# Gate projections of two sequence mixers: wide split products against plain products on four column quarters

## The chip, the cores and the metric

The kernel runs on one core of one Trainium2 chip. The metric is the time of one execution in device microseconds (us); lower is better. The core has a matrix engine (PE, with its weight loads listed apart as PEld), a vector engine (DVE), a scalar engine (ACT), a third elementwise engine (POOL) and a queue engine (SP) that issues most of the transfers. They run side by side and wait for one another at semaphores.

## The reference, cut to what matters

The program is a two-layer encoder trunk over 512 tokens of width 1024, in float32. Layer 0 mixes tokens with forgetting attention and differential attention, layer 1 with a chunkwise mLSTM. Each mixer reads the normalised input and, beside its large projections, a very narrow one: eight gate columns.

```python
xn = rms_norm(x, mix_norm[layer])              # x * rsqrt(mean(x^2) + eps) * gain
proj = xn @ w_in                               # 1024 -> some 3000 columns
# layer 0: ff is 8 of those columns, one for each forgetting head
log_f = log_sigmoid(ff + fox_bf)               # its running sum biases the attention logits
# layer 1: ig and fg are 4 columns each, one for each mLSTM head
i_pre = ig + b_i
log_f = log_sigmoid(fg + b_f)
```

The change concerns only how these 8 + 8 columns, 16 numbers for each token, are computed. Their later use (running sums, maxima, exponentials) stays.

## The kernel before, in words

**Layout.** x is held transposed, as eight tiles of 128 model dimensions by 512 tokens (`x0` to `x7`). A projection is a sum over these eight blocks k.

**Split products.** Float32 operands are split in two: a high part (`xh`, `wh`) in a reduced float type that the matrix engine takes at full rate, and the remainder (`xl`, `wl`). A large product is three matmuls: high times high, high times low, low times high. ACT makes the high part (a cast, line 285), DVE the low part (a subtraction, line 282). For x the gain of the norm is multiplied in at the same time (lines 604 and 605). The root of the mean square is divided out later, when a result is read from its bank (`rb`, the reciprocal root spread over the partitions).

**Weights.** A weight tile of 128 by 1024 arrives by a transfer in `raw`, is split into `wh` and `wl`, and is used by 24 matmuls. There are three `wh` and three `wl` buffers, and tiles take them in turn: a new `wl` waits until the products that read the tile three turns earlier have run.

**Order.** In both mixers a planner (class `Plan`) sets the order in which instructions are written. It holds assumed durations, priorities, and some times before which an item may not start (`after`); the memory work of layer 0 enters at such times (`MEM_AT` = 140 and 95). All engines run their own list in the order written, so one waiting instruction holds everything behind it on its engine.

**The gates.** `p_gate` adds one planner item for each k, of two matmuls: the gate weights against `xh[k]` (line 669) and against `xl[k]` (line 670). The gate weights are split as well, and high and low part lie side by side as columns of one `wh` buffer: 40 columns in layer 0 and 100 in layer 1, with gaps, so that each part begins at a multiple of 32. So there are 16 matmuls over 512 tokens in each layer. `gate_rows` then adds the rows of the two parts (lines 679 and 680), multiplies by `rb` (681) and adds the bias (682); in layer 1 it runs twice, for input and forget gate.

**Around them.** In layer 0 the gates stand among the first products of the program, between the products of the value projection of the differential heads (`dv`, lines 352 to 354, four blocks of 128 tokens at a time), while x is still being prepared. The root of layer 0 runs through lines 588 (sums), 484 to 489 (root), 559 (diagonal tiles) and 565 (two products that spread it). In layer 1 they follow the last product of layer 0's feed-forward block, and the mLSTM's value projection (lines 352 to 354 again) follows them; the norm sums are line 498.

**Other float32 products.** `weigh` of the differential heads (line 814) and of the forgetting heads (line 1033) multiply float32 tiles without a split. Line 1033 does so for two heads at once: 64 columns each, written to partitions 0 to 63 and 64 to 127 of one bank, with a position given for each product:

```python
for s in range(2):
    nc.tensor.matmul(ps[64 * s : 64 * s + 64, j * P : 512], v[j][:, c : c + 64], ...,
        start=(j == 0), stop=(j == 3), tile_position=(0, 64 * s))
```

Of the kernel before, what the change touches and what calls it, by code (L numbers as in the profile page):

```python
# [236 lines left out]
class Builder:  # L237
# [407 lines left out]
    def gate_weights(self, src, m, parts):  # L645

        nc = self.nc
        raw = self.til(self.sp, "gw", (P, 8, m), bufs=1)
# [9 lines left out]
    def p_gate(self, pl, weights, w, evac, kdeps=None, edeps=(), prio=0):  # L658

        st = {}  # L660
        last = None
        for k in range(KB8):

            def fn(k=k):
                if k == 0:
                    st["g"] = weights()
                    st["ps"] = self.bank("w")
                mm = self.nc.tensor.matmul
                mm(st["ps"][:w, :], st["g"][:, k, :], self.xh[k][:], start=(k == 0), stop=False)
                mm(st["ps"][:w, :], st["g"][:, k, :], self.xl[k][:], start=False, stop=(k == 7))  # L670
# [4 lines left out]
    def gate_rows(self, out, ps, hi, lo, n, bias):  # L675

        nc = self.nc
        t = self.til(self.sp, "sqt")[:n, :]
        nc.scalar.copy(t, ps[lo : lo + n, :])
        nc.vector.tensor_tensor(out=t, in0=ps[hi : hi + n, :], in1=t, op=ALU.add)  # L680
        nc.vector.tensor_tensor(out=t, in0=t, in1=self.rb[:n, :], op=ALU.mult)
        nc.vector.tensor_scalar(out=out, in0=t, scalar1=self.col(bias)[:n, :], scalar2=None, op0=ALU.add)
# [1647 lines left out]
```

## Time and profile before

| what | us |
|---|---|
| median of 3 runs (lowest, highest) | 1453.03 (1452.55, 1453.50) |
| the profiled execution, its whole time | 1452.78 |
| its span in the profile | 1451.0 |
| PE busy | 1435.7 (99%) |
| PEld busy | 1276.1 |
| DVE busy | 1223.3 (84%) |
| ACT busy | 992.0 (68%) |

The span is what the instructions of the trace cover; 1.78 us of the profiled execution lie around it. The granted clock of the matrix engine was 0.999. Rows of a timeline give the start in us from the span's start, the duration, the engine, the line, the operation, and the tiles written and read, with their shapes; in brackets stands the idle time before an instruction and what ended it. Matmuls overlap in their pipeline, so the spacing of their starts tells the rate, not the duration of one: a split product of 512 columns takes 0.39 us and the next starts some 0.23 us later. A float32 product without a split leaves two records for each instruction.

### The profile page before, as it was taken

What the parts mean: (1) busy time and instruction counts of PE and PEld (TensorE: products, weight loads), DVE (VectorE), ACT (ScalarE), POOL (GpSimd) and SP (SyncE); (2) the same over time, 40 slices, a digit from 0 to 9 for tenths busy, and PEclk for the clock granted to TensorE, in tenths of its full rate; (3) what the DMA queues carried; (4) which work ended last, traced back from release to release, by engine and by line L of the source; (5) the groups of instructions that cost most, each with busy time, mean ns of one, the idle gap of its engine ahead of it and who ended that gap; (6) DMA issues with size and microseconds to landing.
All of it is one profiled execution on the core that took longest, in us unless ns stands there. A gap on an engine that the chain in (4) does not pass through costs nothing.

```text
span 1451.0 us, 23997 instructions
## 1 busy us (share of the span) xinstructions
PE 1435.7 (99%) x8989; PEld 1276.1 (88%) x8989; DVE 1223.3 (84%) x2171; ACT 992.0 (68%) x1782; POOL 74.7 (5%) x116
## 2 busy tenths in 40 slices
PE   9999999999999999999999999999999999999998
PEld 7888788998889999999888788899888999999987
DVE  7789987877899988888769888887779999888974
ACT  7689766655677777777547676566566777777764
POOL 0001120000000000000000100000000000000000
PEclk9999999999999999999999999999999999999999
DMA  5222336752246655552233323656314666565322
GB/s 201 87 74 73 117 118 209 184 167 79 95 135 163 180 161 158 151 161 74 84 106 109 121 90 102 189 146 174 131 52 124 175 161 174 153 167 153 102 71 75
DMA packets 71062, 190.37 MB, mean 131 GB/s; under 512 B 7825, under 2 KB 7954, under 8 KB 70946
## 3 DMA queue, kind: packets, MB, share of 16 engines
q1 hardware_dynamic: 63170, 162.30, 33.5%
q0 software_dynamic: 7200, 26.22, 10.5%
q8 instruction: 70, 1.15, 0.3%
q14 instruction: 46, 0.38, 0.1%
q10 hardware_dynamic: 576, 0.33, 0.1%
HBM read 186.69 MB, written 2.13 MB: 130 GB/s over the span
## 4 chain that ended last, share of the span: by engine, by line
PE 79%; DVE 12%; ACT 4%; issue 3%; DMA 1%; POOL 0%; DVEq 0%; SPq 0%; POOLq 0%; ACTq 0%
PE acc L291 14%; PE acc L292 14%; PE acc L293 14%; PE w L291 6%; PE w L293 6%; PE w L292 6%; PE s L291 3%; PE s L293 3%; PE s L292 3%; DVE wl L282 2%; PE acc L352 2%; PE acc L354 2%; PE acc L353 2%; DVE hs L1830 1%; DVE x L773 1%
## 5 line engine op out<-in xcount | busy, mean ns | idle before, releaser
L282 DVE TENSOR_TENSOR wl<-raw,wh 128x1024 fp32r<-128x1024 f32 (+3 forms) x181 | 213.7, 1181 | 32.5 <-ACT wh L285 25.8
L291 PE MATMUL acc<-xh,wh 128*128 128x256 f32 (+1 forms) x624 | 207.0, 332 | 0.1
L293 PE MATMUL acc<-xh,wl 128*128 128x256 f32 (+1 forms) x624 | 205.5, 329 | 0.2 <-DVE wl L282 0.2
L292 PE MATMUL acc<-xl,wh 128*128 128x256 f32 (+1 forms) x624 | 205.6, 329 | 0.0
L285 ACT CAST wh<-raw 128x1024 fp32r<-128x1024 f32 (+1 forms) x123 | 126.6, 1034 | 79.3 <-PE acc L292 38.7
L1690 DVE SCALAR_TENSOR_TENSOR c<-hs,vec,c 128x512 f32<-128x512 f32 x176 | 130.6, 747 | 16.6 <-ACT c L1683 14.7
L291 PEld LDWEIGHTS acc<-xh,wh 128*128 128x128 f32 x624 | 117.2, 188 | 12.5 <-ACT v L1931 0.9
L292 PEld LDWEIGHTS acc<-xl,wh 128*128 128x128 f32 x624 | 117.3, 188 | 11.8
L293 PEld LDWEIGHTS acc<-xh,wl 128*128 128x128 f32 x624 | 117.1, 188 | 11.9 <-DVE wl L282 0.6
L291 PE MATMUL w<-ah,wh 128*128 128x512 f32 x304 | 118.7, 391 | 0.5 <-ACT w L1597 0.5
L293 PE MATMUL w<-ah,wl 128*128 128x512 f32 x304 | 119.0, 391 | 0.0
L292 PE MATMUL w<-al,wh 128*128 128x512 f32 x304 | 118.6, 390 | 0.0
L1683 ACT ACTIVATE c<-hs,vec 128x512 f32<-128x512 f32 x88 | 71.0, 815 | 13.0 <-DVE hs L1830 7.3
L282 DVE TENSOR_TENSOR wl<-sa,wh 128x1024 fp32r<-128x1024 f32 x52 | 63.4, 1220 | 17.1 <-ACT wh L1761 15.5
L1761 ACT CAST wh<-sa 128x1024 fp32r<-128x1024 f32 x42 | 44.0, 1048 | 34.6 <-PE w L292 30.8
L293 PEld LDWEIGHTS w<-ah,wl 128*128 128x128 f32 x304 | 57.1, 188 | 12.0
L291 PEld LDWEIGHTS w<-ah,wh 128*128 128x128 f32 x304 | 57.1, 188 | 11.2 <-ACT w L1597 1.4
L1567 ACT CAST wh<-dr 128x512 fp32r<-128x512 f32 x64 | 39.6, 618 | 39.3 <-PE w L292 31.4
L292 PEld LDWEIGHTS w<-al,wh 128*128 128x128 f32 x304 | 57.1, 188 | 9.8
L1746 POOL DMA_DIRECT2D sa<-in_up_dram x42 | 35.9, 856 | 510.4 <-DVE hs L1830 178.7
L282 DVE TENSOR_TENSOR s<-sb,s 128x512 fp32r<-128x512 f32 x88 | 60.2, 684 | 2.0
L291 PE MATMUL acc<-mem,wh 128*128 128x256 f32 (+1 forms) x192 | 61.6, 321 | 0.0
(571 smaller groups left out, 4661.0 us busy)
## 6 DMA issues: line engine op xcount, KB each, us to landing
raw<-in_up_dram SPq DMA_DIRECT2D x46, 512.0 KB, 3.3
sa<-in_up_dram SPq DMA_DIRECT2D x42, 512.0 KB, 4.2
sa<-in_up_dram POOLq DMA_DIRECT2D x42, 512.0 KB, 5.5
dr<-in_down_dram SPq DMA_DIRECT2D x64, 256.0 KB, 2.7
ra<-in_up_dram SPq DMA_DIRECT2D x42, 256.0 KB, 2.8
raw<-in_xk_dram SPq DMA_DIRECT2D x16, 512.0 KB, 3.4
raw<-in_wo_dram SPq DMA_DIRECT2D x16, 512.0 KB, 3.4
raw<-in_xv_dram SPq DMA_DIRECT2D x16, 512.0 KB, 3.2
```

The costliest lines, as they stand in the source:

```text
L282: self.nc.vector.tensor_tensor(out=lo, in0=v, in1=hi.bitcast(F32), op=ALU.subtract)
L285: self.nc.scalar.copy(hi, v)
L291: mm(out, wh, xh, start=first, stop=False, skip_group_check=parts)
L292: mm(out, wh, xl, start=False, stop=False, skip_group_check=parts)
L293: mm(out, wl, xh, start=False, stop=last, skip_group_check=parts)
L352: mm(ps, xh[k][:, ts], wh[:, ws], start=(k == 0), stop=False)
L353: mm(ps, xh[k][:, ts], wl[:, ws], start=False, stop=False)
L1567: nc.scalar.copy(st["wh"][:, :cols], st[tag][:, :cols])
L1683: nc.scalar.activation(st["c_"][:, j, :], hs()[:, j, 2:514], AF.Identity, scale=self.col("cw", (layer * 3 + 2) * 44 + blk), bias=self.col( ...
L1690: nc.vector.scalar_tensor_tensor(out=c, in0=hs()[:, j, n : n + 512], scalar=w, in1=c, op0=ALU.mult, op1=ALU.add)
L1746: return add("POOL", 0.0029 * cols, lambda: nc.gpsimd.dma_start(out(), src(), accum_op=ALU.add), deps, due, (), (), 6.0)
L1761: nc.scalar.copy(s["wh"][:, :cols], raw())
```

## The change

The gates are computed from x itself, without a split of x or of the gate weights. The gain of the norm is multiplied into the weights instead (a product on DVE, over 8 blocks of 8 columns). The weights are padded to 32 columns. The eight blocks k go to four quarters of the columns of the array: k = 0 to 3 to quarters 0 to 3, and k = 4 to 7 again, added to the first. So one bank holds four partial sums, at partitions 0, 32, 64 and 96. This bank is split into two tiles as any other operand is (one cast on ACT, one subtraction on DVE, 128 by 512 each), and two products with a matrix of zeros and ones (`sel`) add the four quarters. `sel` is made by DVE out of the identity, and lies in a `wl` buffer, which the gates did not take before. `gate_rows` becomes one product with `rb` on DVE and one activation with a bias on ACT.

For the planner the items change: two of 0.9 us in place of eight of 0.455 us, then the split, the two sums, and the reading of the rows. The value projection's products with k = 4 and later come after the sums in the plan.

```diff
-    def gate_weights(self, src, m, parts):
+    def gate_weights(self, src, gi, rows):
...
-        both = self.til(self.wp, "wh", (P, 1088), F32R, bufs=3)[:, : 8 * parts[-1][2]].rearrange("p (a b) -> p a b", a=8)
-        nc.vector.memset(both.bitcast(F32), 0.0)
-        for a, hi, lo, n in [(p[0], p[1], p[2] - p[3], p[3]) for p in parts]:
-            h = both[:, :, hi : hi + n]
-            nc.vector.tensor_copy(h, raw[:, :, a : a + n])
-            self.sub(both[:, :, lo : lo + n], raw[:, :, a : a + n], h)
-        return both
+        both, sel = self.parts()
+        w = both[:, :256].bitcast(F32).rearrange("p (a b) -> p a b", a=8)
+        nc.vector.memset(w, 0.0)
+        a = VEC["mix"][0] + 8 * gi
+        nc.vector.tensor_tensor(out=w[:, :, :8], in0=raw[:], in1=self.vec[:, a : a + 8].unsqueeze(2).to_broadcast([P, 8, 8]), op=ALU.mult)
+        m = rows[-1][0] + rows[-1][2]
+        nc.vector.memset(sel[:, :m].bitcast(F32), 0.0)
+        ident = self.ident[:].rearrange("p (a b) -> p b a", b=32)
+        for at, first, n in rows:
+            with nc.allow_low_precision(reason="zeros and ones"):
+                nc.vector.tensor_reduce(out=sel[:, at : at + n], in_=ident[:, first : first + n, :], axis=AX.X, op=ALU.add)
+        return w, sel[:, :m]
...
-        for k in range(KB8):
+        for g in range(2):
...
-                mm(st["ps"][:w, :], st["g"][:, k, :], self.xh[k][:], start=(k == 0), stop=False)
-                mm(st["ps"][:w, :], st["g"][:, k, :], self.xl[k][:], start=False, stop=(k == 7))
-
-            last = pl.add(fn, 2 * MM, [last, *(kdeps or {}).get(k, [])], prio, take=("w",) if k == 0 else ())
-        return pl.add(lambda: evac(st["ps"]), 0, [last, *edeps], prio, free=("w",), chain=(("A", 0.5), ("D", 0.6), ("D", 0.6), ("D", 0.4)))
+                for j in range(4):
+                    at = slice(32 * j, 32 * j + 32)
+                    nc.tensor.matmul(st["ps"][at, :], st["w"][:, 4 * g + j, :], self.x[4 * g + j][:], start=g == 0, stop=g == 1, tile_position=(0, 32 * j))
+
+            ks = [d for k in range(4 * g, 4 * g + 4) for d in (kdeps or {}).get(k, [])]
+            last = pl.add(fn, 0.9, [last, *ks], prio, take=("w",) if g == 0 else ())
+
+        def parts():
+            st["parts"] = [self.til(self.sp, "sqt", dtype=F32R) for _ in range(2)]
+            self.split(st["parts"][0][:], st["parts"][1][:], st["ps"][:])
+
+        def sums():
+            ps = st["sum"] = self.bank("w")
+            for i, part in enumerate(st["parts"]):
+                nc.tensor.matmul(ps[: st["sel"].shape[1], :], st["sel"], part[:], start=i == 0, stop=i == 1)
+
+        a = pl.add(parts, 0, [last], prio, free=("w",), chain=(("A", 0.5), ("D", 0.6)))
+        a = pl.add(sums, 2 * MM, [a], prio, take=("w",))
+        return a, pl.add(lambda: evac(st["sum"]), 0, [a, *edeps], prio, free=("w",), chain=(("D", 0.6), ("A", 0.5)))
...
-        nc.scalar.copy(t, ps[lo : lo + n, :])
-        nc.vector.tensor_tensor(out=t, in0=ps[hi : hi + n, :], in1=t, op=ALU.add)
-        nc.vector.tensor_tensor(out=t, in0=t, in1=self.rb[:n, :], op=ALU.mult)
-        nc.vector.tensor_scalar(out=out, in0=t, scalar1=self.col(bias)[:n, :], scalar2=None, op0=ALU.add)
+        nc.vector.tensor_tensor(out=t, in0=ps[at : at + n, :], in1=self.rb[at : at + n, :], op=ALU.mult)
+        nc.scalar.activation(out, t, AF.Identity, bias=self.col(bias)[:n, :])
...
-            g = self.p_gate(pl, lambda: gw, 40, gates, xk, [norm], 1)
+            gd, g = self.p_gate(pl, lambda: gw, gates, xk, [norm], 1)
+            xk[4].append(gd)
...
-            g = self.p_gate(pl, lambda: self.gate_weights(t["gate1"], 8, [(0, 0, 68, 4), (4, 32, 100, 4)]), 100, gates, edeps=[norm], prio=1)
+            gd, g = self.p_gate(pl, lambda: self.gate_weights(t["gate1"], 1, [(0, 0, H), (32, H, H)]), gates, edeps=[norm], prio=1)
```

In the new kernel the gates' products are line 676 and the sums line 688; lines behind them move down by 17 or 18.

**PE at the start of layer 0.** Before, the last gate products stand around the first four products of `dv` with block k = 2, just ahead of the norm sums (line 588):

```order
L669 MATMUL w_17_191<-xh6_29_229,wh_4_148 40x512
L670 MATMUL w_17_191<-xl6_30_230,wh_4_148 40x512
L669 MATMUL w_17_191<-xh7_31_235,wh_4_148 40x512
L352 MATMUL acc0_18_194<-wh_35_265,xh2_15_185 128x512
L352 MATMUL acc1_19_195<-wh_35_265,xh2_15_185 128x512
L352 MATMUL acc2_20_196<-wh_35_265,xh2_15_185 128x512
L352 MATMUL acc3_21_197<-wh_35_265,xh2_15_185 128x512
L670 MATMUL w_17_191<-xl7_32_236,wh_4_148 40x512
L588 MATMUL s_37_282<-ones2_82,tb_11_173 128x2 x4
L353 MATMUL acc0_18_194<-wl_36_266,xh2_15_185 128x512
```

Now the product with x0 stands alone much earlier, right behind the first four products of `dv`; the other seven stand together ahead of block k = 2, and the first sum (line 688) stands where the last gate product was:

```order
L676 MATMUL w_34_253<-x5_143,wh_4_148 32x512
L676 MATMUL w_34_253<-x6_144,wh_4_148 32x512
L676 MATMUL w_34_253<-x7_145,wh_4_148 32x512
L352 MATMUL acc0_18_193<-wh_36_259,xh2_16_187 128x512
L352 MATMUL acc1_19_194<-wh_36_259,xh2_16_187 128x512
L352 MATMUL acc2_20_195<-wh_36_259,xh2_16_187 128x512
L352 MATMUL acc3_21_196<-wh_36_259,xh2_16_187 128x512
L688 MATMUL w_51_324<-sqt_43_307,wl_5_149 8x512
L588 MATMUL s_38_288<-ones2_82,tb_12_175 128x2 x4
L353 MATMUL acc0_18_193<-wl_37_260,xh2_16_187 128x512
```

The second sum has moved behind the first of the two products that spread the root (line 565), and six products of block k = 4 now stand between those two.

**DVE a little later in layer 0.** Before, the low part of the fourth `dv` weight tile (`wl_60`, blocks k = 6 and 7) stands ahead of the two diagonal tiles of the root (line 559):

```order
L489 SCALAR_TENSOR_TENSOR y_40_289<-a_41_290,y_40_289 128x4
L282 TENSOR_TENSOR wl_60_378<-raw_58_376,wh_59_377 128x1024
L554 CAST rh_42_313<-y_40_289 128x4
L282 TENSOR_TENSOR rl_43_314<-y_40_289,rh_42_313 128x4
L559 TENSOR_TENSOR sqt_45_318<-ident_75,rh_42_313 128x512
L559 TENSOR_TENSOR sqt_46_321<-ident_75,rl_43_314 128x512
```

Now it stands between them (`wl_64`):

```order
L852 TENSOR_REDUCE le_58_351<-tmp_57_349 128x2
L554 CAST rh_45_311<-y_41_295 128x4
L282 TENSOR_TENSOR rl_46_312<-y_41_295,rh_45_311 128x4
L559 TENSOR_TENSOR sqt_48_316<-ident_75,rh_45_311 128x512
L282 TENSOR_TENSOR wl_64_377<-raw_62_375,wh_63_376 128x1024
L559 TENSOR_TENSOR sqt_49_319<-ident_75,rl_46_312 128x512
```

Since `sel` takes a `wl` buffer at the start, `wl_64` takes the buffer of the second `dv` tile (`wl_37`, blocks k = 2 and 3); before, it took that of the first.

**PE among the forgetting heads of layer 0.** The planner's times before which memory work may not start lead to another interleaving from there on. Before, scores (lines 768 and 769), transposes (802) and the next projection alternate:

```order
L802 MATMUL w_1760<-ident,x_141 128x128
L768 MATMUL s_1806<-ka_284_1479,qa_281_1471 128x256
L769 MATMUL s_1806<-kb_116,qa_281_1471 128x256
L291 MATMUL acc_375_1878<-xh_9_168,wh_1873 128x512
L292 MATMUL acc_375_1878<-xl_10_169,wh_1873 128x512
L293 MATMUL acc_375_1878<-xh_9_168,wl_1874 128x512
L802 MATMUL w_1798<-ident,x_139 128x128
L291 MATMUL acc_375_1878<-xh_12_176,wh_1873 128x512
L802 MATMUL w_1801<-ident,x_138 128x128 x2
```

Now, at the same place (scores are lines 785 and 786 and transposes line 819 here):

```order
L785 MATMUL s_1787<-ka_288_1478,qa_285_1470 128x256
L786 MATMUL s_1787<-kb_116,qa_285_1470 128x256
L291 MATMUL acc_382_1886<-xh_10_170,wh_1881 128x512
L819 MATMUL w_1777<-ident,x_139 128x128
L292 MATMUL acc_382_1886<-xl_11_171,wh_1881 128x512
L819 MATMUL w_1780<-ident,x_138 128x128 x2
L785 MATMUL s_1833<-ka_289_1482,qa_286_1473 128x256
L819 MATMUL w_1822<-ident,x_143 128x128 x2
L786 MATMUL s_1833<-kb_118,qa_286_1473 128x256
```

Fewer projection products stand between transposes and scores there. Further on in this stretch the same step of the two heads of a pair often stands back to back.

More of the change, by code (lines that the diff above doesn't have):

```diff
@@ L660, in p_gate, with fn @@
+        for at, first, n in rows:
+            with nc.allow_low_precision(reason="zeros and ones"):
+                nc.vector.tensor_reduce(out=sel[:, at : at + n], in_=ident[:, first : first + n, :], axis=AX.X, op=ALU.add)
+        return w, sel[:, :m]
+    def p_gate(self, pl, weights, evac, kdeps=None, edeps=(), prio=0):
+        nc = self.nc
         st = {}
         last = None
[L662 to L666 removed]
+        for g in range(2):
+            def fn(g=g):
+                if g == 0:
+                    st["w"], st["sel"] = weights()
@@ new lines, in sums, with gate_rows @@
+        def sums():
[5 more added lines that the diff above has]
+        return a, pl.add(lambda: evac(st["sum"]), 0, [a, *edeps], prio, free=("w",), chain=(("D", 0.6), ("A", 0.5)))
+    def gate_rows(self, out, ps, at, n, bias):
@@ L916, in gates @@
                 z = rows["z"] = self.til(self.memp, "mem", bufs=8)[:8, :]
-                self.gate_rows(z, ps, 0, 32, 8, "foxb")
+                self.gate_rows(z, ps, 0, 8, "foxb")
                 self.lam()
@@ L1901, in gates @@
                 zf = self.til(mp, "th")[:H, :]
-                self.gate_rows(zi, ps, 0, 64, H, "bi")
-                self.gate_rows(zf, ps, 32, 96, H, "bf")
+                self.gate_rows(zi, ps, 0, H, "bi")
+                self.gate_rows(zf, ps, 32, H, "bf")
                 f = self.log_sigmoid_sum(zf, H, mp, "mk", "num", "th")
@@ L1946, in mix1 @@
                     self.p_proj_tok(
-                        pl, t["mv"][nh], self.xs, 4, lambda tk, ps, nh=nh: values(tk, ps, nh), edeps=[norm], prio=(2, V1_PRIO)[nh], chain=(("A", 0.52),)
+                        pl, t["mv"][nh], self.xs, 4, lambda tk, ps, nh=nh: values(tk, ps, nh), kdeps={4: [gd]}, edeps=[norm], prio=(2, V1_PRIO)[nh], chain=(("A", 0.52),)
                     )
```

7 lines of the change are left out of this document (2 added, 5 removed).

## The prediction

> **What bounds the kernel now.** I read the page first, then timelines around the two places of the gates, then the waits.
>
> ```profile
> span 1451.0 us, 23997 instructions
> PE 1435.7 (99%) x8989; PEld 1276.1 (88%) x8989; DVE 1223.3 (84%) x2171; ACT 992.0 (68%) x1782; POOL 74.7 (5%) x116
> PE 79%; DVE 12%; ACT 4%; issue 3%; DMA 1%; POOL 0%; DVEq 0%; SPq 0%; POOLq 0%; ACTq 0%
> ```
>
> PE is busy for 99% of the span and holds 79% of the chain that ended last. So time taken off PE is time saved, unless PE must wait at that place for something else. The profiled execution took 1452.78 us, 1.78 more than its span and 0.25 less than the median, 1453.03; a saving s gives a span of 1451.0 - s and a median of 1453.03 - s.
>
> Layer 1 is the plain place. This is the timeline of PE, DVE and ACT from the first gate product on:
>
> ```profile
> 739.07 0.39 PE L669 MATMUL w<-xh,wh 128*100 128x512 f32 x1
> 739.27 0.69 DVE L621 TENSOR_TENSOR x<-w,x 128x512 f32<-128x512 f32 x1 [0.73 <-PE w L293]
> 740.62 0.61 ACT L598 ACTIVATE sqt<-x 128x512 f32<-128x512 f32 x1
> 741.93 0.68 DVE L599 TENSOR_TENSOR sq<-sq,sqt 128x512 f32<-128x512 f32 x1
> 742.77 0.39 PE L352 MATMUL acc<-wh,xh 128*128 128x512 f32 x1
> 745.50 0.39 PE L498 MATMUL s<-rb,ones 128*128 128x512 f32 x1
> ```
>
> The 16 gate products fill 739.07 to 742.77, that is 3.70 us or 0.23 each, and the value projection follows at once. Nothing waits there: this is PE time proper.
>
> The start of layer 0 is another matter. PE:
>
> ```profile
> 13.54 0.39 PE L669 MATMUL w<-xh,wh 128*40 128x512 f32 x1
> 15.60 1.09 PE L352 MATMUL acc<-wh,xh 128*128 128x512 f32 x4
> 16.53 0.40 PE L670 MATMUL w<-xl,wh 128*40 128x512 f32 x1
> 16.77 0.95 PE L588 MATMUL s<-ones,tb 128*128 128x2 f32 x8
> 17.57 0.48 PE L353 MATMUL acc<-wl,xh 128*128 128x512 f32 x1
> 22.24 1.02 PE L565 MATMUL s<-sqt,ones 128*128 128x512 f32 x2
> 23.09 0.39 PE L352 MATMUL acc<-wh,xh 128*128 128x512 f32 x1
> ```
>
> ACT and DVE beside it:
>
> ```profile
> 14.05 1.98 ACT L285 CAST wh<-raw 128x1024 fp32r<-128x1024 f32 x2
> 15.71 1.21 DVE L282 TENSOR_TENSOR wl<-raw,wh 128x1024 fp32r<-128x1024 f32 x1
> 20.00 1.22 DVE L282 TENSOR_TENSOR wl<-raw,wh 128x1024 fp32r<-128x1024 f32 x1
> 21.41 0.69 DVE L559 TENSOR_TENSOR sqt<-ident,rh 128x512 fp32r<-128x512 f32 x1
> 22.01 0.69 DVE L559 TENSOR_TENSOR sqt<-ident,rl 128x512 fp32r<-128x512 f32 x1
> ```
>
> PE runs without a gap, but only just: the weights of block k = 2 (`wh`) are cast from 14.05, the first of two casts ends near 15.05, and the low part near 16.92. Whatever PE saves before is capped there.
>
> **The new products.** A float32 product without a split is in the trace in two forms, with the same columns (512, 384, 256 and 128 in turn): line 814, four products on all 128 columns of the array, and line 1033, eight products, two heads side by side on 64 columns each. The timeline of PE around one of each, with the instruction after it:
>
> ```profile
> 93.23 2.32 PE L814 MATMUL w<-pt,v 128*128 128x512 f32 x8
> 95.30 0.48 PE L768 MATMUL s<-ka,qa 128*128 128x512 f32 x1
> 167.90 2.37 PE L1033 MATMUL w<-pt,v 128*64 128x512 f32 x16
> 170.20 0.33 PE L802 MATMUL w<-ident,x 128*128 128x128 f32 x1
> ```
>
> Start to start, 1280 columns take 2.07 us on the whole array (1.62 ns a column, 0.83 us for 512), and twice the products on halves take 2.30 us. So halves do run at once: one after the other, they would take 4.14. For a pair of 512 columns that is 0.92 us (512 / 1280 x 2.30). No row shows four quarters. From below, all four at once: 0.92 for a group of four, 1.84 for both. From above, no overlap at all: 8 x 0.83 = 6.62. Between them, two at once: 4 x 0.92 = 3.68. I take 1.84, by the nearest row, line 1033, where a neighbour on other columns costs 11%.
>
> The Trainium skill ("TensorE: Matmul & The Clock Gate", section "Measured speedup vs the span model") gives 2.38 times for three column tiles with 512 columns, not three; at that efficiency (0.79), an estimate, a group of four would take 4 x 0.83 / 3.17 = 1.05 us and layer 1 would save 0.26 less. The pair here reaches 1.80 of 2, somewhat better, so the sum stays with the row.
>
> **Layer 1, worked out.** Removed 3.70 us; added 1.84 and two sums of 0.23 (the spacing of the L669 rows) = 0.46. The last x tile is added by L621 until 739.96, when the second group starts; its three other products can go first, so I cost that at nothing (0.1 without that cover). The split of the bank: the cast follows L598 on ACT, 741.23 to 741.85 (0.61, as L598); the subtraction follows L599 on DVE, 742.6 to 743.3 (0.69, as L559). The sums stand behind 12 projection products, 739.07 + 1.84 + 12 x 0.23 = 743.7, so they do not wait; if DVE were later, PE would lose just that. The norm's sums (L498) go from 745.50 to about 746.8, since 12 more products stand ahead of them, but the value projection's 96 products (21.8 us) cover the root. Saving: 3.70 - 1.84 - 0.46 = **1.4 us**.
>
> **Layer 0, worked out.** Block k = 1 ended before at 13.54. Six gate products ahead of it go (1.4), and the lone product with x0 comes (0.83, and 0.1 to change over): PE is there at 13.1. Seven products, in two groups, 1.84: 14.9. Then PE waits for the cast of `wh`, 15.05, and starts at 15.1 instead of 15.60. Four products (0.93): 16.0. First sum, 0.23; its cast ends on ACT at 15.05 + 0.61, earlier. L588 as before, 0.80: L353 starts at 17.05, just after its `wl`, instead of 17.57. That is 0.5 saved of the 1.8 that the products are shorter; the rest becomes the wait at 15.
>
> Then 20 products, 4.6 us: L565 at 21.7; its diagonal tile is early enough (0.5 sooner, plus 0.6 for the new subtraction on DVE, minus 1.2 for the `wl` that moved behind it). Second sum, 0.23, then six products, 1.4: 23.4. The second L565 needs the second diagonal tile, which stands on DVE behind the moved `wl`; that `wl` now waits for the products of block k = 3, which end near 21.9: 21.9 + 1.2 + 0.6 = 23.7, so PE waits 0.3 and is through at 24.0. Six products later than in the old order, this compares with 23.09 + 1.4 = 24.45. Saving: **0.4 us**; bounds: 0 (that chain 0.4 later) and 1.3 (no wait anywhere: 16 x 0.23 - 1.84 - 0.46).
>
> **The smaller edits.** The split of the gate weights goes and a product with the gain and two small reductions come; these lie on DVE far ahead of their use. In `gate_rows` DVE loses about 1.1 us in layer 0 and twice that in layer 1:
>
> ```profile
> 24.66 0.67 DVE L680 TENSOR_TENSOR sqt<-w,sqt 8x512 f32<-8x512 f32 x1
> 25.36 0.68 DVE L681 TENSOR_TENSOR sqt<-sqt,rb 8x512 f32<-8x512 f32 x1
> 26.08 0.47 DVE L682 TENSOR_SCALAR mem<-sqt,vec 8x512 f32<-8x512 f32 x1
> ```
>
> PE does not wait for that here (0 in the sum). **The other order** among the forgetting heads has no price of its own in the trace. That stretch before, and the longest waits of PE there and in the mLSTM:
>
> ```profile
> 165.00:230.00 65.00, 64.32 (x389) 52.06 (x388) 52.77 (x142) 40.73 (x88) 13.76 (x22) 1.00 0.43 141
> PE w L802 <- ACT pt L805: 0.7, 1, 0.7
> PE s L498 <- DVE mk L2036: 1.2, 1, 1.2
> ```
>
> PE is busy 64.32 of 65.00 us. All that the new order could win is 0.7; it could lose that wait of 0.7 several times. I take 0 and keep -0.7 and +1.4 (two such waits).
>
> **Sum.** 1.4 + 0.4 = 1.8 us: a span of 1449.2, an execution of 1451.0, a median of **1451.2 us**. A measurement of this kernel tells 0.2%, 2.9 us, from no change; so this counts as no change. The likeliest case's own range is 1450.2 to 1452.8.
>
> **Rivals.**
>
> *More than the PE time.* The rows of gates are done earlier in layer 1, by 2.2 us of DVE work; they lead to the mLSTM's maxima and scores. If the 1.2 us wait of L498 for DVE (L2036) goes as well: 1450.0; with the 0.7 of the other stretch, 1449.3. For it: DVE holds 12% of the chain. Against it: that wait comes some 70 us later, behind other work.
>
> *Two quarters at a time.* Two float32 streams is the most that the trace shows. Layer 1 then loses 3.68 + 0.46 - 3.70 = 0.4. In layer 0 seven products take 3.2 instead of 1.84, PE comes to block k = 2 at 16.3 instead of 15.1, and loses 1.2 - 0.4 = 0.8: 1454.2. Against it: halves cost only 11% for their neighbour.
>
> *No overlap.* With quarters one after the other, layer 1 loses 6.62 + 0.46 - 3.70 = 3.4, and layer 0 3.4 as well (13.1 + 7 x 0.83 = 18.9 against 15.1, less 0.4): 1459.8. Line 1033 speaks against it. This is also the case in which the change does not do what it says.
>
> *The other order costs more than the gates save: slower.* Place: PE among the forgetting heads, 165 to 230 us. With the same step of both heads back to back, a transpose meets its bank not yet copied, each time at the price of the row above, 0.7. It decides from the third wait (2.1 against 1.8); with seven, 4.9, the time is 1456.1, over 0.2% slower. For it: two banks serve all transposes, and the new order brings them closer together. Against it: only one such wait stood in the whole old order.
>
> **How the numbers follow.** Forecast 0.62; more than the PE time 0.16; two at a time 0.10; the other order 0.09; no overlap 0.03. Faster by over 0.2% (below 1450.1): most of the second case and a tail of the first, 0.17. Slower by over 0.2% (above 1455.9): the last, most of the fourth, little of the third, 0.11. Within: 0.72. The range, 1449.4 to 1454.5, holds the first three and leaves out most of the others.
>
> **What would show it.** In the changed profile, layer 1 should show eight products of line 676 in 1.8 to 2.0 us, with starts in groups of four; 3.7 would be two at a time and 6.6 none. In layer 0 block k = 2 should start at 15.1, behind a short wait for ACT, its low part at 17.05, and the second L565 near 23.7, behind DVE. If block k = 4 is reached no earlier than before, the saving of layer 0 is wrong; if the stretch from 165 to 230 changes by more than 1 us, it is the order that sets the result, and not the gates.

## The result, and the profile after

The changed kernel takes 1454.96 us (median of 22 runs, 1452.81 to 1459.86), the kernel before 1453.32 (22 runs beside them, 1452.55 to 1453.77). The ratio is 1.0013, with a 95% interval of 1.0007 to 1.0019: slower by 1.6 us in the medians (1.0 to 2.8 by the interval), where 1.8 us less was forecast. The profiled execution took 1455.62 us.

From the page of the changed kernel:

```profile
span 1453.8 us, 24006 instructions
PE 1435.5 (99%) x8993; PEld 1274.6 (88%) x8993; DVE 1221.7 (84%) x2168; ACT 992.7 (68%) x1784; POOL 75.3 (5%) x116
```

and from its list of PE's waits (us in total, times, longest):

```profile
PE s L1935 <- DVE cv L1923: 1.9, 1, 1.9
...
PE acc L352 <- ACT wh L285: 0.8, 1, 0.8
```

PE looks as busy as before. Two waits matter and are new: one of 1.9 us for line 1935, and one of 0.8 us at the start of layer 0. A third new one, of 0.7 us at line 291 near 1157 us, costs nothing: against the kernel before, PE is 2.9 us late at 1130 us and 3.0 at 1160.

**Layer 1.** The timeline of PE in the changed kernel, from the gates on:

```profile
740.28 0.39 PE L293 MATMUL w<-ah,wl 128*128 128x512 f32 x1
740.60 1.92 PE L676 MATMUL w<-x,wh 128*32 128x512 f32 x16
742.45 0.50 PE L352 MATMUL acc<-wh,xh 128*128 128x512 f32 x1
742.79 0.39 PE L353 MATMUL acc<-wl,xh 128*128 128x512 f32 x1
...
745.31 0.62 PE L688 MATMUL w<-sqt,wl 128*36 128x512 f32 x2
...
748.55 0.39 PE L498 MATMUL s<-rb,ones 128*128 128x512 f32 x1
...
770.56 0.39 PE L293 MATMUL acc<-xh,wl 128*128 128x512 f32 x1
772.81 0.41 PE L1935 MATMUL s<-ident,cv 4*128 4x4 f32 x4 [1.86 <-DVE cv L1923]
773.14 0.50 PE L291 MATMUL acc<-xh,wh 128*128 128x512 f32 x1
...
774.83 0.63 PE L291 MATMUL acc<-xh,wh 128*128 128x512 f32 x1
775.25 0.63 PE L292 MATMUL acc<-xl,wh 128*128 128x512 f32 x1
```

The products do what was forecast: 740.60 to 742.45 is 1.85 us for the eight. Going over to the quarters and back costs 0.2 us beside that: 0.32 us lie between the product before and the first on quarters, and 0.34 between the first two behind, where 0.23 is usual. Then comes what was not. Line 1935 turns the finished gate rows into columns by four small transposes; it is line 1917 of the kernel before. PE starts the product ahead of them at 770.56 and them at 772.81, where 0.23 later was due: a wait of 2.0 us. (Waits are counted in this way here; the 1.86 in brackets begins at the modelled end of the product.) Behind them the products stand 0.43 us apart instead of 0.23. The same stretches by window (after the length of the window come busy time and count of PE, PEld, DVE, ACT and POOL, then the granted clock, the share of DMA and the GB/s):

```profile
771.00:774.40 3.40, 1.59 (x9) 1.37 (x10) 3.40 (x5) 2.66 (x3) 0.00 (x0) 1.00 0.36 126
774.40:777.80 3.40, 3.40 (x9) 2.67 (x8) 3.39 (x7) 1.34 (x2) 0.00 (x0) 0.50 0.11 40
777.80:781.20 3.40, 3.40 (x16) 2.81 (x15) 2.56 (x4) 0.90 (x2) 1.39 (x2) 1.00 0.76 257
```

PE was busy for less than half of the first window, was granted half its clock for all of the second, and the full clock again in the third. The trace has the half clock from 774.40 to 777.81, 3.41 us.

Why is the wait there? The chain to the transposes, on DVE in the kernel before, with the transposes themselves:

```profile
752.29 0.69 DVE L532 SCALAR_TENSOR_TENSOR rb<-asumh,sq 128x512 f32<-128x512 f32 x1
...
769.71 0.67 DVE L1905 TENSOR_TENSOR cv<-cv,th 4x512 f32<-4x512 f32 x1
...
771.00 0.41 PE L1917 MATMUL s<-ident,cv 4*128 4x4 f32 x4
```

and on DVE in the changed one:

```profile
755.69 0.69 DVE L532 SCALAR_TENSOR_TENSOR rb<-asumh,sq 128x512 f32<-128x512 f32 x1
...
772.08 0.67 DVE L1923 TENSOR_TENSOR cv<-cv,th 4x512 f32<-4x512 f32 x1
```

Before, the rows were done at 770.38, 0.6 us before PE came. Now they are done at 772.75. From the root (`rb`) on, the chain is 1.0 us shorter (17.40 to 16.37), as the shorter `gate_rows` promised. But the root is 3.4 us later, since line 498 has gone from 745.50 to 748.55: 12 products more stand between the gates and it. And PE comes to the transposes sooner, by what the products save.

**Layer 0.** ACT and PE at the start of the changed kernel:

```profile
5.83 0.72 ACT L604 ACTIVATE xh<-x,vec 128x512 fp32r<-128x512 f32 x1 [0.77 <-DMA x<-in_x_dram]
...
14.81 1.03 ACT L285 CAST wh<-raw 128x1024 fp32r<-128x1024 f32 x1
...
13.23 1.92 PE L676 MATMUL w<-x,wh 128*32 128x512 f32 x14
15.89 1.18 PE L352 MATMUL acc<-wh,xh 128*128 128x512 f32 x4 [0.75 <-ACT wh L285]
...
17.95 0.48 PE L353 MATMUL acc<-wl,xh 128*128 128x512 f32 x1
...
24.52 0.51 PE L565 MATMUL s<-sqt,ones 128*128 128x512 f32 x1
```

The second x tile reached ACT at 5.83 here and at 5.07 in the profile before, and everything on ACT moved with it.

**Where the time went.** The starts of the same instruction in both traces, subtracted, give how far a kernel is behind the one before (minus: ahead). Places are times of the kernel before; `E` are the experiments below.

| kernel | 34 | 225 | 737 | 770 | 772 | 800 | 839 | 850 | end |
|---|---|---|---|---|---|---|---|---|---|
| changed | 0.4 | 1.5 | 1.4 | -0.1 | 1.8 | 3.4 | 2.7 | 2.7 | 2.8 |
| changed, profiled again (E15) | -0.2 | 0.8 | 0.6 | -1.0 | 1.1 | 2.6 | 1.9 | 2.2 | 2.4 |
| layer 1 alone (E2) | 0.3 | 0.5 | 0.6 | -1.0 | 1.0 | 1.0 | 0.6 | 0.6 | 1.4 |
| changed, root sooner (E14) | -0.3 | 0.8 | 1.1 | -0.4 | -0.4 | -0.4 | -1.9 | -0.7 | -0.4 |
| changed, root sooner, old head order (E13) | 0.3 | 0.6 | 0.3 | -1.2 | -1.2 | -1.2 | -2.5 | -1.6 | -1.4 |
| layer 1 alone, root sooner (E11) | -0.3 | 0.2 | 0.2 | -1.3 | -1.3 | -1.3 | -1.6 | -0.7 | -0.6 |
| old gates, root sooner (E16) | 0.2 | 0.5 | 0.3 | 0.1 | 0.1 | 0.1 | -1.7 | -0.7 | -0.3 |

Both profiles of the changed kernel agree: 1.0 lost from 34 to 225 us; 1.6 gained from 737 to 770 us; 1.9 to 2.1 lost in the wait for the transposes; 1.5 to 1.6 lost at half clock; 0.6 to 0.7 given back by 839, of which 0.2 to 0.3 at line 498.

Of the 1.6 gained, 1.1 is there by 749 us, behind the gates and their sums: 3.70 for the old products, less 1.85 for the new ones, 0.2 for going over and back, and 0.5 for the sums. Another 0.3 comes at 765 us, where the kernel before has a short wait of its own: its weight load for line 291 stands until ACT has read the values out (line 1931). PE and PEld before:

```profile
764.79 0.39 PE L354 MATMUL acc<-wh,xl 128*128 128x512 f32 x1
765.32 0.50 PE L291 MATMUL acc<-xh,wh 128*128 128x512 f32 x1
...
765.32 0.19 PEld L291 LDWEIGHTS acc<-xh,wh 128*128 128x128 f32 x1 [0.57 <-ACT v L1931]
```

In the changed kernel the same two products stand the usual 0.23 apart (765.12 and 765.35), and in E16, with the old gates, as well (765.36 and 765.59). So this 0.3 does not come from the shorter products. The last 0.1 to 0.2 come right behind it.

### The profile page after: what moved, and what is told of

Its sections match the earlier page's. It is cut to its first block, busy times and chain, and to the rows that moved or that the text cites. A ratio compares the mean times of both kernels' runs of the same rounds, so it can differ in the third digit from the quotient of the medians.

```text
span 1453.8 us, 24006 instructions
## 1 busy us (share of the span) xinstructions
PE 1435.5 (99%) x8993; PEld 1274.6 (88%) x8993; DVE 1221.7 (84%) x2168; ACT 992.7 (68%) x1784; POOL 75.3 (5%) x116
## 4 chain that ended last, share of the span: by engine, by line
PE 81%; DVE 10%; ACT 5%; issue 2%; DMA 1%; POOL 0%; SPq 0%; DVEq 0%; ACTq 0%; POOLq 0%
PE acc L291 15%; PE acc L292 15%; PE acc L293 15%; PE w L291 6%; PE w L293 6%; PE w L292 6%; PE s L291 3%; PE s L292 3%; PE s L293 3%; PE acc L352 2%; PE acc L354 2%; PE acc L353 2%; DVE wl L282 2%; DVE c L1708 1%; DVE hs L1848 1%
```

## The experiments

Runs of one group shared a chip and runs of the kernel before. "Low clock" counts runs whose mean granted clock was 0.998 or less. In the 120 runs of the kernel before beside E1 to E16 there is none. Every span ends at half clock (1.0 to 4.2 us of it in the profiles), which enters this mean: by itself it makes 0.9985 or more, together with one more window of 3.41 us less than that. So the sign separates the two, but narrowly. The interval is that of the ratio; of the kernels with a sooner root, only E11's lies wholly below 1.

| run | median us | before us | difference | ratio, 95% | low clock |
|---|---|---|---|---|---|
| changed | 1454.96 | 1453.32 | +1.64 | 1.0007 to 1.0019 | 15 of 22 |
| E1 layer 0 alone | 1454.60 | 1453.84 | +0.76 | 0.9998 to 1.0016 | 1 of 11 |
| E2 layer 1 alone | 1454.12 | 1453.84 | +0.28 | 0.9992 to 1.0009 | 6 of 11 |
| E3 transposes later | 1453.80 | 1453.84 | -0.04 | 0.9993 to 1.0011 | 1 of 11 |
| E6 old head order | 1454.70 | 1453.84 | +0.86 | 0.9997 to 1.0015 | 9 of 11 |
| E7 layer 1 alone, transposes later | 1453.01 | 1453.37 | -0.36 | 0.9987 to 1.0005 | 0 of 10 |
| E8 before, no last tap | 1452.85 | 1453.37 | -0.52 | 0.9989 to 1.0007 | 0 of 11 |
| E9 as E7, no last tap | 1453.17 | 1453.37 | -0.20 | 0.9991 to 1.0009 | 4 of 11 |
| E10 before, longer row chain | 1453.95 | 1453.37 | +0.58 | 0.9995 to 1.0013 | 0 of 10 |
| E11 layer 1 alone, root sooner | 1451.59 | 1453.36 | -1.77 | 0.9979 to 0.9996 | 0 of 11 |
| E12 before, longer row chain still | 1455.43 | 1453.36 | +2.07 | 1.0004 to 1.0023 | 0 of 11 |
| E13 both, root sooner, old head order | 1451.80 | 1453.36 | -1.56 | 0.9983 to 1.0001 | 0 of 11 |
| E14 both, root sooner | 1452.20 | 1453.60 | -1.40 | 0.9983 to 1.0000 | 0 of 11 |
| E15 changed, again | 1455.52 | 1453.60 | +1.92 | 1.0006 to 1.0024 | 8 of 11 |
| E16 before, root sooner | 1452.28 | 1453.60 | -1.32 | 0.9983 to 1.0001 | 0 of 11 |

### E1 and E2: one layer at a time

```diff
-            gd, g = self.p_gate(pl, lambda: self.gate_weights(t["gate1"], 1, [(0, 0, H), (32, H, H)]), gates, edeps=[norm], prio=1)
+            g = self.p_gate_old(pl, lambda: self.gate_weights_old(t["gate1"], 8, [(0, 0, 68, 4), (4, 32, 100, 4)]), 100, gates, edeps=[norm], prio=1)
...
-            gd, g = self.p_gate(pl, lambda: gw, gates, xk, [norm], 1)
+            g = self.p_gate_old(pl, lambda: gw, 40, gates, xk, [norm], 1)
```

The first pair of lines, with the old functions under the names `_old`, makes E1 of the changed kernel, the second E2.

> The new gates in layer 0 alone; layer 1 as before. The two traces put the changed kernel 0.4 us behind the old one at 25 us, 1.5 behind at 230 us, still 1.4 behind at 737 us, level again at 766 us, and 3.4 behind at 780 us, after a wait of PE for the transposes of the gate rows and a stretch at half clock. Theory W (the wait in layer 1 and the clock after it decide): this kernel has neither, keeps what is lost up to 230 us at most, and is within 0.2 to 1.5 us of the kernel before: 1453.5 to 1454.8. Rival O (layer 0 decides, its start and the other order among the forgetting heads): the full 1.5 and nothing else of note, 1454.8, so nearly the whole of the changed kernel's loss. In both the profile should show 1.5 lost by 230 us if that loss repeats, and a clock of 1 throughout the span but for its end.

> The new gates in layer 1 alone; layer 0 as before, and with it the old order among the heads. Theory W: 1.5 us gained by the products, 1.9 lost in the wait for the transposes of the gate rows, 0.7 gained at the later wait of the norm sums, 1.6 lost to a window at half clock of about 3.4 us where there is one: 1453.0 without the window and 1454.7 with it, and so runs of this kernel spread by 1.6 us as those of the changed kernel do. Rival O: with layer 0's loss gone and the wait and the clock of no weight of their own, faster than before by the 1.4 us that the products save: 1451.9.

E1, at +0.76, lies within theory W's 0.2 to 1.5; the rival's 1.5 is missed by half in the median, but its interval reaches 2.3. E2, at +0.28, refutes the rival, which had it 1.4 us faster: layer 1 saves at the gates and is behind again at 772 us. PE in the profile of E2:

```profile
769.72 0.39 PE L293 MATMUL acc<-xh,wl 128*128 128x512 f32 x1
771.96 0.40 PE L1973 MATMUL s<-ident,cv 4*128 4x4 f32 x4 [1.86 <-DVE cv L1961]
```

and the window behind it:

```profile
773.60:777.00 3.40, 3.40 (x17) 2.79 (x16) 3.39 (x7) 1.36 (x2) 0.00 (x0) 1.00 0.18 58
```

The same wait, and this time no half clock behind it. So the wait brings the window in some executions only; by the mean clock, 6 of 11 runs of E2 had it. In E2 these runs were no longer than the rest (median 1454.10 against 1454.13), where theory W had them 1.7 us longer. Why they are not is open.

### E3 and E7: the transposes later

```diff
-            uc = pl.add(ucols, 0.4, [g], 2, take=("s",), free=("s",), chain=(("D", 0.1),))
+            ug = pl.add(lambda: None, 0, [g], 2, chain=(("L", 2.0),))
+            uc = pl.add(ucols, 0.4, [ug], 2, take=("s",), free=("s",), chain=(("D", 0.1),))
```

> The changed kernel with one more item in layer 1's plan, which puts the four transposes of the gate rows (line 1935) 12 products, 2.7 us, later on PE; nothing else moves but these. Theory W: the wait of 1.9 us goes, and with it the window at half clock of 3.4 us that costs 1.6: about 1451.5 to 1452.5, with no spread beyond that of the kernel before. Rival N (the wait only moves on: what is late is the whole chain of the gate rows, and the scores that need them wait instead): 1454 to 1455, with a new wait of some 2 us of PE behind line 1935. Rival C (the clock falls for another reason, the products on quarters of the array): a window at half clock still shows at 740 to 750 us or later, and the time is 1453.1 or more.

> The new gates in layer 1 alone, with the transposes of the gate rows 12 products later; layer 0 as before. Theory D (between the gates and the norm sums that wait at 828 us PE is paced by the work of DVE and ACT, so that what it saves in front is waited for there): the wait at 770 us is gone, PE is 1.4 us ahead at 772 us, and level with the kernel before again by 840 us; the time is that of the kernel before, within 0.4 us. Rival P (PE's time is what counts once the wait is gone): 1.4 us ahead at 840 us and to the end, so 1.4 us faster than before.

Wait and window are gone (1 low run of 21), though all the products on quarters remain: these alone do not lower the clock. But the time is only level with the kernel before, as theory D had it for E7; theory W's 1451.5 to 1452.5 for E3 was missed, and rival N was half right. Rival P is not refuted by E7's time (the interval reaches 1.9 us faster) but by its profile, where PE is 1.6 us ahead at 787 us and 0.2 at 800. The next wait in E3, PE:

```profile
787.66 0.39 PE L293 MATMUL acc<-xh,wl 128*128 128x512 f32 x1
788.93 0.50 PE L291 MATMUL s<-qh,kh 128*128 128x512 f32 x1 [0.88 <-ACT kh L1989]
```

`kh` is the first convolved key. Its convolution begins by multiplying with `rb` and stands on DVE behind the rows of the gates. The late root makes this late too; with the sooner root of E11 and E14 the wait does not come (nothing is lost from 772 to 800 in the table).

### E6: the old order among the forgetting heads

```diff
-            last = pl.add(fn, 0.9, [last, *ks], prio, take=("w",) if g == 0 else ())
+            last = pl.add(fn, dur, [last, *ks], prio, take=("w",) if g == 0 else ()) 
```

`dur` is 1.2 in layer 0 and stays 0.9 in layer 1.

> The changed kernel with 1.2 us in place of 0.9 as the planner's duration of a group of gate products in layer 0; from 25 us on PE's order in layer 0 is then again that of the kernel before, row by row. If the other order among the forgetting heads costs the 1.07 us that the traces show between 60 and 230 us, this kernel is 1.1 us faster than the changed one: 1453.9. If that loss came from elsewhere (the rows of the gates reaching the heads late, a transfer), it stays at 1455.0, with the same 1.5 us lost by 230 us.

Between 34 and 225 us E6 loses 0.4 us, where the changed kernel loses 1.0. Over all profiles: five with the new order lose 1.0 to 1.1 there, ten with the old one 0.2 to 0.5. So the order costs about 0.7 on PE. The time agrees in size (+0.86, where the changed kernel, on other chips, has +1.64 and +1.92); but between E13 and E14, which differ in this alone, the differences to the kernel before are only 0.2 apart (on two chips). What it costs at the end stays between 0.2 and 1.1.

### E8 and E9: less work for DVE

```diff
-                for tap in (2, 1, 0):
+                for tap in (2, 1):
```

Both kernels leave out the last tap of the mLSTM's convolution, 6.2 us of products on DVE.

> The kernel before without the last tap of the mLSTM's convolution (eight products of DVE of 0.77 us, 6.2 us, left out; the planner's costs and so the order of all else as before). Theory D: the waits of PE among the mLSTM's heads that DVE ends (1.2 us at the norm sums, some of the 2.3 us at the convolution's input) shrink, and the time falls by 1 to 2.5 us against the kernel before. Rival P: PE is busy there anyway; less than 0.5 us.

> The new gates in layer 1 alone, with the transposes later, and without the same tap. To be compared with the kernel before without that tap. Theory D: with 6.2 us less on DVE the products' saving gets through: at 840 us PE is ahead of the other kernel by 1.0 to 1.4 us, and the time is lower by as much. If something else takes the saving away (a transfer, a bank, the chain of the gate rows), the two are level within 0.4 us.

Theory D missed in both times: E8 gained 0.5 and not 1 to 2.5, and E9 is not below E8 but 0.3 above it, which is the other case named for E9 (level within 0.4). In E8 PE does gain 1.3 us at line 498 near 830, and then waits 1.2 for the evacuation of the second half of the values on ACT (line 1931):

```profile
845.93 0.34 PE L293 MATMUL s<-qh,kl 128*128 128x384 f32 x1
847.33 0.50 PE L291 MATMUL acc<-xh,wh 128*128 128x512 f32 x1 [1.06 <-ACT v L1931]
```

In E9 the lead of the gates passes 787 us without a wait (0.8 ahead from 776 to 813), as theory D had it, and is lost at 814, in a wait of 2.1 us for DVE (ACT had stood idle for 4.3 us there until a transfer landed; this was not followed further):

```profile
816.59 0.50 PE L352 MATMUL acc<-wh,xh 128*128 128x512 f32 x1 [1.96 <-DVE hs L2013]
```

The window behind it:

```profile
817.30:820.70 3.40, 3.40 (x11) 2.84 (x10) 2.48 (x4) 2.02 (x4) 0.10 (x1) 0.51 0.87 264
```

A window at half clock again, 75 us behind the last product on quarters.

### E10 and E12: a longer wait with the old gates

```diff
+                nc.vector.tensor_tensor(out=mx, in0=zi, in1=f, op=ALU.subtract)
...
+            g0 = pl.add(lambda: None, 0, [g], 1, chain=(("L", 4.5),))
...
-            uc = pl.add(ucols, 0.4, [g], 2, take=("s",), free=("s",), chain=(("D", 0.1),))
+            uc = pl.add(ucols, 0.4, [g0], 2, take=("s",), free=("s",), chain=(("D", 0.1),))
```

The first line runs once in E10 and three times in E12.

> The kernel before, with its old gates, but with the transposes of the gate rows 9 products (2.05 us) earlier on PE and one more subtraction on DVE (0.67 us, to a tile that is written later anyhow) in their chain, so that PE waits some 2.1 us for them. No product runs on a quarter of the array. If a wait of 2 us is enough to bring a window at half clock, about half of the runs show a mean clock of 0.998 or less, as with the changed kernel, where 55 runs of the kernel before show none; the time is 0.5 to 2.5 us above the kernel before. If the products on quarters bring it, all runs show 0.999 or more.

> The kernel before, old gates, with the transposes 9 products earlier as in the last run of this kind, and three more subtractions on DVE instead of one, so that PE waits about 2.7 us for them instead of 1.4. Ten runs with a wait of 1.4 us had a mean clock of 0.999 throughout. If a wait of 2 us or more brings the window at half clock, at least half of the runs show 0.998 or less; if products on quarters are needed for it, none does. The time is 1 to 2.5 us above the kernel before.

Neither made the wait it was meant to make. In the built programs the transposes stood 3 products earlier (E10) and 8 later (E12), not 9 earlier, and PE waited 1.4 us in both. In E12:

```profile
772.97 0.39 PE L292 MATMUL acc<-xl,wh 128*128 128x512 f32 x1
774.63 0.41 PE L1919 MATMUL s<-ident,cv 4*128 4x4 f32 x4 [1.28 <-DVE cv L1908]
```

No run of the 21 had a low clock. E12 is slower by 2.1 us without a low clock; its profile shows waits of 1.4 us here and 1.0 more at 789 and 791. The old gates with a wait of 2 us were not had, so what they would do to the clock was not tried.

### E11, E13, E14, E15 and E16: the root sooner

```diff
-            norm = self.x_norm(pl, (mp, "asumh", 1), 0, after=3.5, cols=True)
+            norm = self.x_norm(pl, (mp, "asumh", 1), 0, after=1.5, cols=True)
+            norm = pl.add(lambda: None, 0, [norm], 0, chain=(("L", 2.0),))
```

The last line (3.0 in E16) keeps the plan's later times, so that line 498 moves and little else does. E13 has E6's edit too; E15 is the changed kernel as it was.

> The new gates in layer 1 alone, and the norm's sums (line 498) 12 products earlier on PE, that is 12 products behind the gates, where they stood before the change; the rest of PE's order is that of the run with layer 1 alone. Theory D: the rows of the gates and the convolutions start when DVE has the reciprocal root; this now comes some 3 us sooner, so the wait of 2.0 us for the transposes goes (the last subtraction ends near 769.5, before PE is there at 770), the wait of 1 us for kh that came in its place does not come, and PE is 1.4 us ahead at 800 us. Behind that the wait of the norm sums at 828 us can take up to 1.4 of it. Time: 0.5 to 1.5 us below the kernel before. Rival: DVE has as much work as ever, and PE is level again by 800 us: the time of the kernel before.

> The whole change, with the two corrections together: 1.2 us as the planner's duration of a group in layer 0, which gives the old order among the heads, and the norm's sums of layer 1 12 products earlier. Theory (the losses are the order among the heads, 0.7, and the wait with the clock in layer 1): as the run with the norm's sums earlier and layer 1 alone, within 0.5 us, since layer 0 then neither gains nor loses. If the start of layer 0 loses by itself (a wait for ACT of 0.8 us, one of 0.5 us at the second product that spreads the root), it is 0.5 to 1.0 us slower than that.

> The whole change with the norm's sums of layer 1 12 products earlier, and nothing else: the order among the forgetting heads is the changed kernel's. If that order costs 0.7 us on PE (150 to 230 us, in four profiles), this kernel is 0.5 to 1.0 us slower than the one with both corrections, and loses 0.8 us between 150 and 225 us against the kernel before. If the order is of no weight for the time, the two are level within 0.3. No run below 0.999, since the wait of 2 us is gone.

> The changed kernel itself once more, on the same chip as the two beside it. If wait, clock and order are what it loses: 3.0 to 3.5 us slower than the kernel with both corrections, that is 1.4 to 2.0 above the kernel before, and at least half of its runs at 0.998 or less. If the chip of the first comparison was the cause, it is level with the kernel before here.

> The kernel before, old gates in both layers, with the norm's sums of layer 1 some 10 products earlier on PE and the rest of its order kept. Theory D: no wait for the gate rows stands in this kernel that a sooner root could take away, but for 0.3 us at 765 us; 0 to 0.5 us faster than the kernel before. Rival G (what the corrected kernels gain comes from the sooner root and not from the gates): 1.0 to 1.8 us faster, as they are.

E14 and E15 differ in this edit alone and shared a chip: 1452.20 against 1455.52. The place of two norm sums is worth 3.3 us to the changed kernel, and E15, at +1.92 with 8 low clocks, repeats the first comparison on this chip. PE and DVE in E14:

```profile
745.00 0.39 PE L498 MATMUL s<-rb,ones 128*128 128x512 f32 x1
...
770.55 0.41 PE L1936 MATMUL s<-ident,cv 4*128 4x4 f32 x4
...
753.24 0.69 DVE L532 SCALAR_TENSOR_TENSOR rb<-asumh,sq 128x512 f32<-128x512 f32 x1
...
768.76 0.67 DVE L1924 TENSOR_TENSOR cv<-cv,th 4x512 f32<-4x512 f32 x1
```

The rows are done 1.1 us before PE comes; no wait, no low clock in 33 runs of E11, E13 and E14. E11 is 1.8 us faster than the kernel before (0.9979 to 0.9996).

E16 is the sobering one. The old gates with the sooner root are 1.3 us faster as well, by the wait of line 498 near 830 that goes (the lead at 839 in the table). So of the 3.3 us, 1.3 has nothing to do with the gates, and rival G holds for most of the gain: E11, E13 and E14 gain 0.1 to 0.5 more than E16, on other chips in part, and their intervals overlap. Whether the short products are worth anything at the end is left open by the times. The profiles show where such a lead is thinned out: whoever comes early to 845 us waits there for ACT,

```profile
844.70 0.34 PE L293 MATMUL s<-qh,kl 128*128 128x384 f32 x1
846.27 0.50 PE L291 MATMUL acc<-xh,wh 128*128 128x512 f32 x1 [1.24 <-ACT v L1950]
```

The wait in brackets is 1.2 us in E14, 0.9 to 1.0 in E11, E13 and E16.

## Why the prediction was wrong

**The new products: right.** 1.85 us for eight was forecast as 1.84, from the pair of line 1033. The estimate from the Trainium skill ("TensorE: Matmul & The Clock Gate", section "Measured speedup vs the span model"), 1.05 us for a group of four, would have had 2.1 for both; the trace is better than the skill's figure for three tiles: eight products of 0.83 us in 1.85 are 3.6 at a time.

**Layer 1's saving: its size right by luck, and wrong in what it reaches.** 1.4 was forecast, and both profiles show it by 765 us; but only 1.1 of it is the gates'. The sum had no term for going over to the quarters and back, 0.2 here, though layer 0's working has 0.1 for going over. The other 0.3 is the wait for ACT at 765 that the kernel before has, and which the sum did not know. Line 498 was forecast at 746.8; taking off the 1.4 us by which the changed kernel was behind there, it came at 747.1. The step that failed is the next one: "the value projection's 96 products (21.8 us) cover the root". They cover the root, but not what hangs on it. The rows of the gates need `rb`, and PE needs the rows at line 1917, 0.6 us after they were ready. Nothing in the prediction followed that chain: it looked at `gate_rows`, found them shorter on DVE, and put them at nothing ("PE does not wait for that here (0 in the sum)"). That term came to 2.0 us of wait. Its sentence that the rows "are done earlier in layer 1, by 2.2 us of DVE work" had the sign wrong: they were 2.4 us later (772.75 against 770.38), and PE came 0.2 us sooner (770.8 against 771.0) although it had been 1.4 behind. Less the 0.6 of slack, that is the wait of 2.0.

**The clock: not foreseen.** The prediction had a wait cost its own length. Here it also cost 1.5 to 1.6 us of half clock in both profiles, and by the mean clock in most executions. By runs, the changed kernel without the low clock is level with the kernel before (median of 7 runs 1453.42 against 1453.32; E15, 3 runs, 1453.49 against 1453.60), and with it 1455.47 (15 runs) and 1456.28 (8). That is a correlation within one kernel, and E2 and E6 don't show it in their times, so the split between wait and clock is shown by the profiles and not by the times.

**Layer 0: forecast 0.4 saved, about nothing.** The working took the cast of `wh` at 14.05 from one execution. In 16 profiles it begins between 13.90 and 14.95, in most of them moved along with the second x tile, which reaches ACT between 5.07 and 6.46, and in all but the profile before, block k = 2 starts 1.1 to 1.2 us after it, with old gates and new. With the old gates PE comes there with ACT or up to 0.5 us ahead of it; with the new ones it waits 0.3 to 1.5. Shorter products only lengthen that wait. In the single profile before, PE started block k = 2 only 0.5 us after the cast allowed it (15.60, where 14.05 and 1.1 make 15.1), and that 0.5 was all there was to gain. At 34 us the kernels with new gates in layer 0 are 0.15 us further behind on average than those with the old ones, less than either group's own spread. The forecast times (15.1, 17.05, 23.7) came as 15.89, 17.95 and 24.52.

**The other order: inside its bounds.** 0 was taken, with -0.7 to +1.4; PE loses 0.7. The rival that named it had the place and the kind of wait, but it needs more of them than there are to decide: 0.4, 0.4, 0.4 and 0.2 us between 150 and 232 us, where 0.7 and 0.2 stood before. That makes 0.5; what makes the rest of the 0.7 is not shown.

**Two at a time, no overlap:** both refuted by the 1.85. **More than the PE time:** it rested on rows that come earlier; they come later. Line 498 near 830, which it wanted gone, did shrink from 1.3 to 1.0, with PE later there and not the rows sooner.

**The sum.** Forecast 1.8 saved. In the profile: 1.6 saved by 770 us in layer 1, and lost 1.9 by the transposes, 1.6 by the clock and 1.4 by the start of layer 0 (0.4) and its heads (1.0); 0.7 came back by 839. Together that is 2.6, or 2.7 before rounding, of the 2.8 behind at the end. The median is only 1.6 behind; by E15 the start of layer 0 alone differs by 0.6 between two executions. The failed step is the one that put the gate rows at nothing: PE waits for them, and they wait for a root that the new order makes 3.4 us later. No rival covered it: the one that spoke of these rows had them early.

## What to carry to other kernels

Removing work from the busiest engine moves it sooner to every later meeting with the others, and the slack at these meetings is what it may gain: here the rows had 0.6 us to spare at the first, and the change moved PE 0.2 sooner and the rows 2.4 later. Follow what the removed work delivered to its consumer, and ask whether the planner still puts the consumer's other input (here a norm of two products) where it was. And look first at the meetings: in this kernel one edit to the place of that norm was worth 1.3 us without any change to the gates (0.9983 to 1.0001).

## What the hardware showed

A wait of PE of 2.0 us in the middle of a busy stretch was followed by 3.41 us at half the clock, some 1.6 us lost, in three of four profiles (the changed kernel, E15 and E6, but not E2), and one of 2.1 us in a fifth (E9). Kernels with one wait of about 2 us (the changed one, E2, E6, E9, E15) had low clocks in 42 of 66 runs; those with waits up to 1.4 us in that place or none (E1, E3, E7, E8, E10 to E14, E16) in 2 of 108.

The Trainium skill ("TensorE: Matmul & The Clock Gate", section "What's actually happening") states half the clock after an idle window of about 3.4 us, and windows that run freely. The trace agrees with the half and the length; but 2.0 us of idle time was enough here, with PE busy for 1.59 of the 3.40 us ahead of the drop. The traces also show that the windows do not begin with the wait. The half clock in the middle begins 675.84 us (the changed kernel and E6), 679.25 (E15) and 631.46 (E9) ahead of the half clock at the end of the span: 198, 199 and 185 times 3.4133 us. Counted back in the same steps from the end of E2's span, where the half clock begins at 1450.67, its wait falls across two windows:

```profile
768.01:771.42 3.41, 2.09 (x10) 1.40 (x8) 3.41 (x5) 3.41 (x6) 0.00 (x0) 1.00 0.00 0
771.42:774.83 3.41, 2.87 (x15) 2.41 (x16) 3.41 (x6) 1.40 (x2) 0.00 (x0) 1.00 0.51 156
```

PE is idle for 1.3 us of one and 0.5 of the other, against 1.8 of one window in the changed kernel. How much idle time a window takes is not settled: near the end of E8 one with PE busy for 1.54 of 3.41 us was followed by the full clock.

Four float32 products on four column quarters start within 0.02 us of each other, and a group takes 0.92 us (1.85 / 2), where one alone takes 0.83; going over to them and back took 0.2 us more. Four neighbours cost each other no more than the two of line 1033 did.
